# Two stacked transformer networks on one core: filler shares replanned, attention's output banks taken later, half down tiles stacked

## The chip, the core and the metric

The kernel runs on one core of one Trainium2 chip. The metric is device time of one execution in microseconds (us), smaller is better. The core has a matmul engine (TensorE; PE in the profile, its weight loads PEld), a vector engine (DVE), an activation engine (ACT), and DMA queues that SyncE (SP) issues to. Engines run their own instruction lists in order and meet at semaphores; the matmul engine too, so a matmul that waits holds up every matmul written behind it.

## The reference

256 tokens of 1024 features pass a first network of two layers and then a second one of two layers; a context of 256 tokens passes the second network beside them, up to the keys and values that the last attention reads. Cut to what matters:

```python
def first_block(x, ...):
    for i in range(2):
        x = layer_norm(ALPHA * x + 0.5 * swiglu(x, gate1[i], up1[i], down1[i]), ...)   # hidden width 2752
        x = layer_norm(ALPHA * x + hybrid_mixer(x, ...), ...)        # four kinds of attention
        x = layer_norm(ALPHA * x + 0.5 * swiglu(x, gate2[i], up2[i], down2[i]), ...)
        x = x + sigmoid(x @ ple_w_gate[i] + b) * (p[i] @ ple_w_proj[i])

def second_block(x, c, ctx, c_ctx, ...):
    for i in range(2):
        m_lat, m_ctx = silu(c) @ ada_w[i] + ada_b[i], silu(c_ctx) @ ada_w[i] + ada_b[i]   # 9 vectors each
        x   = x   + 0.5 * gt1 * swiglu_2(modulate(x,   g1, sh1, sc1), wi, wo)             # hidden width 2816
        ctx = ctx + 0.5 * cg1 * swiglu_2(modulate(ctx, g1, ch1, cs1), wi, wo)
        # i == 0: a conformer convolution (width 31) on x and on ctx
        # i == 1: windowed attention; x reads its own and the context's keys and values
        p = softmax(concat([s_win, s_ctx, sinks]))                     # one sink logit per head
        x = x + gt2 * y;  x = x + 0.5 * gt3 * swiglu_2(modulate(x, g3, sh3, sc3), wi, wo)
        # ctx does the same while i == 0
    return rmsnorm(x, final_g)
```

## The kernel before

Activations lie features by tokens in eight chunks of 128 features. Every large product is made in three matmuls of 128x128 weights on 256 tokens, `mm3` (L741): the weight tile and the input are each split into a rounded part and a rest (`split`, L625, one ACT copy and one DVE subtraction per 128x1024 tile), and the three products that matter are added in PSUM. Weights come from HBM as one packed tile per 24 matmuls.

**Streams.** The program is a set of generators. The main stream runs x through fifteen stages, and `self.phase` counts them: 1 to 4 are feed-forward 1, mixer, feed-forward 2 and gated projection (PLE) of layer 0 of the first network, 5 to 8 the same of layer 1; 9 is the second network's first feed-forward, 10 the front of its convolution, 11 the convolution's taps, norm and projection, 12 and 13 feed-forwards, 14 the attention, 15 the last feed-forward. Inside a mixer or the attention further streams of the same rank do heads in parallel. Two *filler* streams stand beside it: the context stream (`ctx_stream`, matmuls whose input is an `f` or `fh` buffer) and the ada stream (`ada`, L1028: 96 groups of four products, eight matmul records each, that read a 768 KB slab of `ada_w` from one of two buffers `a`). A third kind of work, the convolution's taps, is DVE work alone, put in wherever DVE would idle (`tap`).

**Who goes next** is decided before the program is built: `plan` runs all generators against a cost model (`Model`) and `choose` (L679) writes the list of steps, which the build replays. The main stream goes while its next matmul's operands are ready within 40 ns of the modelled clock; where it isn't, filler goes. Beside that, each microsecond of main work in stage k earns FILLS[k] us of credit (L37), which is spent on filler even though main work is ready. So FILLS moves filler out of one stage's bulk into it, and with it decides how much filler is left for the waits behind. The ada stream is held in layer 1 before group HOLD_G (L1052) until the attention starts.

**Half tiles.** The hidden width 2752 is 21.5 tiles. In the first network's feed-forwards the last piece has 64 rows; `ffn_main` (L786) multiplies it with weights cut to 64 rows (`k=rows` in `mm3`), three matmuls per output chunk, and goes between pieces of 128 and of 64 rows output pair by output pair.

**Attention.** `attention2` (L1702): three workers do eight head pairs. `scores` (L1738) takes two PSUM banks per half, adds the mask (DVE), exponentiates with a running sum (ACT), and exponentiates the sink of each half and head by itself. The output product accumulates in four of the eight PSUM banks, taken when the first pair (flag `a0`) is done.

Of the kernel before, what the change touches and what calls it, by code (L numbers as in the profile page):

```python
# [14 lines left out]
OP = mybir.AluOpType  # L15
# [21 lines left out]
FILLS = (0.25, 0.1, 0.05, 0, 0, 0.05, 0.08, 0, 0.5, 0.25, 0.08, 0.08, 0.05, 0.4, 0.25, 0.05, 0, 0.1)  # L37
# [7 lines left out]
HOLD_G = 5  # L45
# [7 lines left out]
TAP_SLACK = 400  # L53

# [228 lines left out]
class Model:  # L283


    def __init__(self):
        self.clock = [0.0] * 4
        self.table = None
        self.busy = [0.0] * 4
        self.cold, self.window, self.activity = True, 0, 0.0  # L290

# [37 lines left out]
    def pe(self, cost, rows, reads, writes):  # L329

        start = max(self.clock[PE], self.need(PE, reads, writes))
# [61 lines left out]
class WTile:  # L393
# [3 lines left out]
    def h(self, j, m=128):  # L397
        return self.hi[:, j * 128:j * 128 + m]

    def l(self, j, m=128):  # L400
        return self.lo[:, j * 128:j * 128 + m]
# [54 lines left out]
class Prog:  # L456
# [84 lines left out]
    def mms(self, group, cost=None, rows=None):  # L541

        if self.model:
            yield self.model.need(PE, [v for g in group for v in g[1:3]], [g[0] for g in group])
        else:
            yield 0.0
        self.mms_now(group, cost, rows)

    def mms_now(self, group, cost=None, rows=None):
# [8 lines left out]
        m.pe(cost or sum(m.pe_cost(l, r, r.n) for _, l, r, _, _ in group), rows, reads, writes)  # L558
# [182 lines left out]
    def mm3(self, ps, t, j, xh, xl, start, stop, m=128, k=128):  # L741
        wh, wl = t.h(j, m), t.l(j, m)
        if k != 128:
            wh, wl, xh, xl = wh[:k], wl[:k], xh[:k], xl[:k]
        yield from self.mms([(ps, wh, xh, start, False), (ps, wh, xl, False, False), (ps, wl, xh, False, stop)])
# [56 lines left out]
    def ffn_main(self, R, xs, kind, l, acc):  # L802
# [3 lines left out]
        def down(ps):  # L806
# [3 lines left out]
            for b in range(4):  # L810
                for (f, th, rows, key), t in zip(ps, ts):
                    for n in (2 * b, 2 * b + 1):
                        yield from self.mm3(acc[b][:, n % 2], t, n, th[:, 0], th[:, 1], f == 0 and n % 2 == 0,
                                            f == NFB - 1, k=rows)
# [4 lines left out]
        for f in range(NFB):  # L819
# [7 lines left out]
            if uk is None:  # L827
# [6 lines left out]
                self.hidden(ps[:64, 0], u[:64], False, s[:64], h[:64], hh[:64], hl[:64])  # L834
# [11 lines left out]
    def ffn_keys(self, kind, l, f):  # L846
        r0 = f * 128
        if kind in ("ffn1", "ffn2"):
            g, u, d = kind + "_w_gate", kind + "_w_up", kind + "_w_down"
            if f == NFB - 1:  # L850
# [4 lines left out]
                return tuple(key), None, rows_tile(d, l, r0, DFF), 64  # L855
# [176 lines left out]
    def ada(self, l):  # L1032
# [26 lines left out]
        for g in range(6):  # L1059
# [3 lines left out]
            for kc in range(8):  # L1063
# [4 lines left out]
                                     for j in range(4)], 704.0)  # L1068
# [52 lines left out]
    def mixer(self, l, xs, acc):  # L1121
# [221 lines left out]
        def softmax(P, sm, ng, qk, cost=930.0):  # L1343
# [38 lines left out]
        def values(T, O, cols, start=True, stop=True):  # L1382
# [3 lines left out]
                                   for i in range(2)], 860.0)  # L1386
# [31 lines left out]
        def fox(w, j):  # L1418
# [14 lines left out]
            yield from softmax(P, sm, ng, qk, 1760.0)  # L1433
# [298 lines left out]
    def attention2(self, x, xs, G):  # L1732
# [24 lines left out]
        def scores(w, c, P):  # L1757
# [4 lines left out]
            for qb in range(2):  # L1762
# [9 lines left out]
                yield from self.mms(group, 1160.0, 128)  # L1772
                for p, ps in enumerate(pss):
# [26 lines left out]
        def pair(w, c):  # L1800
# [5 lines left out]
            for p in range(2):  # L1806
# [3 lines left out]
                                  T[:, p, kb], kb == 0, kb == 3) for kb in range(4) for p in range(2)], 2230.0)  # L1810
# [254 lines left out]
```

## Time and profile before

| | |
|---|---|
| time, median of 3 runs | 2953.66 us (2950.4 to 2954.9) |
| the profiled execution | 2951.42 us, its span 2949.3 us |
| mean granted matmul clock | 0.976 of full |
| PE busy, PEld busy | 2847.2 us (97%), 2689.1 us (91%) |
| DVE, ACT busy | 1960.3 us (66%), 1407.1 us (48%) |
| DMA | 553.91 MB, 188 GB/s over the span |

All times below are counted from the span's start. A stretch's granted clock is 1.00 at 2.4 GHz and 0.50 at 1.2 GHz; a mean between them is a mix of the two.

### The profile page before, as it was taken

The numbers are of one execution on the slowest core, as the hardware profiler recorded it, in microseconds if no ns is written. First come the engines' busy times: TensorE is split into PE (matmuls) and PEld (weight loads), VectorE is DVE, ScalarE is ACT, GpSimd is POOL, SyncE is SP. The second block draws the span as 40 slices with busy tenths as digits, with TensorE's granted clock in tenths as the row PEclk, the third lists the DMA queues.
The fourth block names the chain that finished last, engine by engine and source line by source line (L and its number), as shares of the span: only waits on it lengthen the run. The fifth ranks groups of instructions, "written<-read, shape, count | busy, mean of one in ns | idle before, by whom it ended". The sixth has DMA issues, their size and how long they took to land.

```text
span 2949.3 us, 55792 instructions
## 1 busy us (share of the span) xinstructions
PE 2847.2 (97%) x23184; PEld 2689.1 (91%) x23184; DVE 1960.3 (66%) x3423; ACT 1407.1 (48%) x2212; POOL 0.2 (0%) x4
## 2 busy tenths in 40 slices
PE   8999999999999999999899989999999999988898
PEld 8999879999999877999799879989999999966898
DVE  5456776557555676755899989987556555666554
ACT  4345445445444544544544444446445444554543
POOL 0000000000000000000000000000000000000000
PEclk9999999999999999999899989999999999989999
DMA  8766645654565555555655665565655555531453
GB/s 289 276 228 209 210 156 173 201 186 162 194 193 164 201 209 194 177 186 183 229 181 184 211 205 198 179 201 190 198 181 177 196 185 187 200 133 45 142 190 111
DMA packets 152845, 553.91 MB, mean 188 GB/s; under 512 B 16272, under 2 KB 26256, under 8 KB 152464
## 3 DMA queue, kind: packets, MB, share of 16 engines
q1 hardware_dynamic: 151728, 548.30, 55.9%
q8 instruction: 182, 2.98, 0.4%
q10 hardware_dynamic: 864, 2.05, 0.2%
q14 instruction: 71, 0.58, 0.1%
HBM read 549.24 MB, written 1.05 MB: 187 GB/s over the span
## 4 chain that ended last, share of the span: by engine, by line
PE 87%; DVE 5%; DMA 4%; ACT 3%; issue 1%; SPq 0%; ACTq 0%; DVEq 0%
PE p L553 86%; DMA a<-ada_w 2%; DVE w L481 1%; PE p L570 1%; ACT k L475 1%; DMA r<-W 1%; DVE m L481 1%; ACT w L475 1%; DVE p L517 1%; ACT m L475 1%; ACT f L475 0%; DMA m_cE<-lam 0%; DVE k L488 0%; DVE m L496 0%; DMA a<-phi_v 0%
## 5 line engine op out<-in xcount | busy, mean ns | idle before, releaser
L553 PE MATMUL p<-m,w 128*128 128x256 f32 x10896 | 1393.1, 284 | 9.1 <-ACT w L475 5.7
L553 PEld LDWEIGHTS p<-m,w 128*128 128x128 f32 x10896 | 1339.6, 190 | 34.2 <-issue 13.1
L481 DVE TENSOR_TENSOR w<-r,w 128x1024 fp32r<-128x1024 f32 (+1 forms) x884 | 1057.9, 1216 | 427.0 <-ACT w L475 416.1
L475 ACT ACTIVATE w<-r 128x1024 fp32r<-128x1024 f32 (+1 forms) x884 | 901.2, 1045 | 435.0 <-PE p L553 336.5
L553 PE MATMUL p<-k,w 128*128 128x256 f32 x4224 | 553.0, 283 | 0.0
L553 PEld LDWEIGHTS p<-k,w 128*128 128x128 f32 x4224 | 524.7, 188 | 8.8 <-issue 4.4
L553 PE MATMUL p<-f,w 128*128 128x256 f32 x3600 | 489.9, 286 | 0.0
L553 PEld LDWEIGHTS p<-f,w 128*128 128x128 f32 x3600 | 454.9, 191 | 10.4 <-issue 4.0
L475 ACT ACTIVATE k<-p 128x256 f32<-128x256 f32 (+1 forms) x200 | 80.6, 403 | 421.8 <-PE p L553 420.9
L553 PE MATMUL p<-fh,w 128*128 128x256 f32 x1776 | 243.3, 284 | 0.2 <-ACT k L475 0.2
L553 PEld LDWEIGHTS p<-fh,w 128*128 128x128 f32 x1776 | 223.7, 190 | 7.2 <-issue 4.2
L481 DVE TENSOR_TENSOR k<-k,p 128x256 f32<-128x256 f32 x176 | 74.0, 420 | 210.3 <-ACT k L475 210.0
L481 DVE TENSOR_TENSOR k<-k,k 128x256 fp32r<-128x256 f32 (+1 forms) x176 | 74.9, 426 | 85.3 <-ACT k L475 85.3
L475 ACT ACTIVATE k<-k 128x256 fp32r<-128x256 f32 (+1 forms) x176 | 73.7, 419 | 108.4 <-DVE k L481 108.4
L553 PE MATMUL p<-a,csf 128*32 128x384 f32 x768 | 93.0, 569 | 30.6 <-DMA a<-ada_w 30.4
L475 ACT ACTIVATE m<-m 128x512 f32<-128x512 f32 (+4 forms) x121 | 64.2, 548 | 81.3 <-DVE m L481 39.9
L496 DVE SCALAR_TENSOR_TENSOR m<-m,vec,m 128x241 f32<-128x241 f32 (+14 forms) x240 | 100.6, 472 | 0.0
L496 DVE SCALAR_TENSOR_TENSOR f<-fh,vec,f 128x241 f32<-128x241 f32 (+14 forms) x240 | 99.9, 473 | 0.0
L553 PEld LDWEIGHTS p<-a,csf 128*32 128x32 f32 x768 | 16.9, 115 | 57.0 <-DMA a<-ada_w 40.3
L475 ACT ACTIVATE k<-p,m_qn 128x128 f32<-128x128 f32 x96 | 39.0, 419 | 60.3 <-DVE m_qn L517 60.3
L517 DVE CUSTOM_DVE_ANT_0 p<-p,masksb 128x128 f32<-128x128 f32 (+2 forms) x128 | 56.0, 453 | 14.9 <-PE p L553 13.3
L475 ACT ACTIVATE f_sq<-p 128x256 f32<-128x256 f32 x66 | 24.9, 378 | 82.3 <-PE p L553 81.9
(219 smaller groups left out, 1428.3 us busy)
## 6 DMA issues: line engine op xcount, KB each, us to landing
r<-W SPq DMA_DIRECT2D x876, 512.0 KB, 4.2
a<-ada_w SPq DMA_DIRECT2D x96, 768.0 KB, 4.9
a<-phi_k SPq DMA_DIRECT2D x8, 512.0 KB, 6.5
a<-phi_v SPq DMA_DIRECT2D x8, 512.0 KB, 4.0
m<-xT SPq DMA_DIRECT2D x4, 256.0 KB, 4.9
r<-W SPq DMA_DIRECT2D x8, 128.0 KB, 4.7
f<-ctxT ACTq DMA_DIRECT2D x1, 1024.0 KB, 10.0
out<-m SPq DMA_DIRECT2D x4, 256.0 KB, 2.5
```

The lines of the kernel that those rows point to most:

```text
L475: self.nc.scalar.activation(out, in_, func, **kw)
L481: self.nc.vector.tensor_tensor(out=out, in0=a, in1=b, op=op)
L496: self.nc.vector.scalar_tensor_tensor(out, a, s, b, op0=op0, op1=op1)
L517: self.nc.vector.tensor_tensor_reduce(ps, ps, mask, -1.0, 3e38, OP.add, OP.min, ng)
L553: self.nc.tensor.matmul(out, l, r, start=start, stop=stop, skip_group_check=True)
L570: self.nc.tensor.transpose(out, in_, ident[:k, :k])
```

## The change

It does four things. The diff is cut to them; lines that only pass arguments or lower a cost in the model are left out.

```diff
-FILLS = (0.25, 0.1, 0.05, 0, 0, 0.05, 0.08, 0, 0.5, 0.25, 0.08, 0.08, 0.05, 0.4, 0.25, 0.05, 0, 0.1)
+FILLS = (0.25, 0.196, 0.025, 0.0, 0, 0.05, 0.08, 0.8, 0.25, 0.02, 0.18, 0.112, 0.18, 0.49, 0.175, 0.05, 0, 0.1)
-HOLD_G = 5
+HOLD_G = 4
+A2_ACC = 2
+TURN = 95.0
...
+    def turned(self, mode):
+
+        t = TURN if mode != self.mode else 0.0
+        self.mode = mode
+        return t
...
-        m.pe(cost or sum(m.pe_cost(l, r, r.n) for _, l, r, _, _ in group), rows, reads, writes)
+        mode = (min(g[1].t.shape[1] for g in group), min(-(-g[1].n // 32) for g in group))
+        turn = m.turned(tuple(x if x < 3 else 4 for x in mode))
+        m.pe(turn + (cost or sum(m.pe_cost(l, r, r.n) for _, l, r, _, _ in group)), rows, reads, writes, need)
...
-                        yield from self.mm3(acc[b][:, n % 2], t, n, th[:, 0], th[:, 1], f == 0 and n % 2 == 0,
-                                            f == NFB - 1, k=rows)
+                        o, last = acc[b][:, n % 2], f == NFB - 1
+                        if rows == 128:
+                            yield from self.mm3(o, t, n, th[:, 0], th[:, 1], f == 0 and n % 2 == 0, last)
+                        else:
+
+                            yield from self.mms([(o, t.h(n), th[:, 0], False, False), (o, t.l(n), th[:, 1], False, last)])
...
-                self.hidden(ps[:64, 0], u[:64], False, s[:64], h[:64], hh[:64], hl[:64])
+                self.hidden(ps[:64, 0], u[:64], False, s[:64], h[:64], hh[:64], hh[64:])
+                self.act(hl[:64], h[:64])
+                self.ts(hl[64:], u[:64], 0.0, None, OP.mult)
...
-                return tuple(key), None, rows_tile(d, l, r0, DFF), 64
+                return tuple(key), None, rows_tile(d, l, r0, DFF) + (piece(d, l, r0, DFF, 0, D, 64),), 64
...
-                    self.act(es[:, p, qb:qb + 1], sk[p], AF.Exp, bias=n1)
+                    self.tt(es[:, p, qb:qb + 1], sk[p], n1, OP.add)
                     R.banks.put(ps)
+            self.act(es, es, AF.Exp)
...
             if c == 0:
+                yield from self.until(f"a{A2_ACC}")
                 for _ in range(4):
                     acc.append((yield from R.bank()))
```

1. **Half pieces stacked.** The 64 weight rows are packed twice, one below the other, and the input's rounded part and its rest fill the two halves of one 128-row operand. Two matmuls of 128 rows do what three of 64 did: 64 stand for 96 in the four feed-forwards, 32 fewer in all. One ACT copy and one DVE multiplication are added to each of the four.
2. **Sinks merged.** Per head pair one ACT exponential of four numbers stands for four of one, and four DVE additions of one column are new.
3. **Banks later.** The four banks of the output product are taken after the third pair (`a2`) is done.
4. **Replanning.** New shares, HOLD_G, and a model that charges 95 ns where the matmuls' tiling changes. No work is added or dropped by it, but nearly every step of every engine stands elsewhere. Filler that stands in the stretches which the prediction speaks of, counted from the program's order (ctx in matmul records, ada in groups):

| stretch | ctx before | ada before | ctx after | ada after |
|---|---|---|---|---|
| stage 6, from the last differential scores to the last forgetting head | 145 | 14 | 174 | 11 |
| stages 7 to 8, from the layer norm's first sum to PLE's first product | 75 | 3 | 0 | 8 |
| stage 10, from stage 9's last product to the convolution's first | 0 | 6 | 147 | 2 |
| stage 11, its start to the context's next gate product | 192 | 9 | 0 | 2 |
| stage 14, last query product to first scores | 175 | 5 | 0 | 0 |
| stage 14, first scores to last output product | 0 | 1 | 0 | 13 |

Matmul engine, the layer norm between stage 7 and stage 8, before. `con` as second operand sums a norm's squares, `m_nr` is its result being transposed, `f` is the context stream, `a` with `csf` the ada stream, `m` with `w` the main stream:

```order
L553 MATMUL p_362_15675<-f_6_12476,w_832_15544 128x256
L553 MATMUL p_362_15675<-f_6_12476,w_831_15543 128x256
L553 MATMUL p_362_15675<-f_7_12477,w_831_15543 128x256
L553 MATMUL p_362_15675<-f_6_12476,w_832_15544 128x256
L553 MATMUL p_303_12550<-a_70_12621,csf 32x384 x4
L553 MATMUL p_303_12550<-a_71_12690,csf 32x384 x4
L570 MATMUL p_363_15745<-con,m_nr_15732 128x128 x2
L553 MATMUL p_303_12550<-a_72_15766,csf 32x384 x4
L553 MATMUL p_365_15806<-m_44_15777,w_833_15607 128x256
```

And the same norm after; `m_41` with `con` are its four partial sums:

```order
L562 MATMUL p_361_15860<-m_41_15858,con 128x256 x2
L562 MATMUL p_362_15868<-a_66_15869,csf 32x384 x4
L562 MATMUL p_361_15860<-m_41_15858,con 128x256 x2
L562 MATMUL p_362_15868<-a_67_15875,csf 32x384 x4
L562 MATMUL p_361_15860<-m_41_15858,con 128x256 x2
L562 MATMUL p_362_15868<-a_68_15887,csf 32x384 x4
L562 MATMUL p_361_15860<-m_41_15858,con 128x256 x2
L562 MATMUL p_362_15868<-a_69_15900,csf 32x384 x4
L562 MATMUL p_362_15868<-a_70_15913,csf 32x384 x4
L562 MATMUL p_363_15936<-con,m_42_15859 128x2 x4
L562 MATMUL p_362_15868<-a_71_15941,csf 32x384 x4
L581 MATMUL p_364_15970<-con,m_nr_15957 128x128 x2
```

The context's products have left this norm; ada groups stand one by one between its steps.

Matmul engine, the norm at the head of stage 10, before: from stage 9's last product (`k` with `w`) to the convolution's first (`m` with `w`):

```order
L553 MATMUL p_384_16507<-k_259_18477,w_984_18480 128x256
L553 MATMUL p_379_16314<-a_81_16294,csf 32x384 x4
L553 MATMUL p_379_16314<-a_82_16315,csf 32x384 x4
L553 MATMUL p_379_16314<-a_83_18675,csf 32x384 x4
L553 MATMUL p_404_18670<-con,m_51_18651 128x2 x4
L570 MATMUL p_405_18687<-con,f_row_16312 128x128 x3
L553 MATMUL p_379_16314<-a_84_18681,csf 32x384 x4
L570 MATMUL p_406_18712<-con,m_nr_18699 128x128 x2
L553 MATMUL p_379_16314<-a_85_18719,csf 32x384 x4
L553 MATMUL p_379_16314<-a_86_18725,csf 32x384 x4
L553 MATMUL p_407_18763<-m_52_18731,w_985_18512 128x256
```

And after, around the transposes of `m_nr`; `fh` is the context's convolution output:

```order
L562 MATMUL p_410_18879<-fh_8_17416,w_995_18761 128x256
L562 MATMUL p_410_18879<-fh_9_17417,w_995_18761 128x256
L562 MATMUL p_410_18879<-fh_8_17416,w_996_18762 128x256
L581 MATMUL p_409_18856<-con,m_nr_18843 128x128 x2
L562 MATMUL p_410_18879<-fh_8_17416,w_995_18761 128x256
```

The context's projection fills this norm from end to end, and the ada groups have left it but for two.

Matmul engine, the attention's first scores, before (`m_of` and `fh` are keys, `m_68` queries, `f_19` with `con` a transposed probability block):

```order
L553 MATMUL p_586_29903<-fh_22_29765,m_68_28986 128x256
L553 MATMUL p_562_29055<-a_112_29746,csf 32x384 x4
L553 MATMUL p_587_29916<-m_of_28987,m_68_28986 128x256
L553 MATMUL p_588_29917<-m_of_28987,m_68_28986 128x256
L553 MATMUL p_587_29916<-fh_22_29765,m_68_28986 128x256
L553 MATMUL p_588_29917<-fh_22_29765,m_68_28986 128x256
```

And after:

```order
L562 MATMUL p_568_29358<-a_103_29847,csf 32x384 x4
L562 MATMUL p_590_29875<-m_of_29348,m_68_29347 128x256
L562 MATMUL p_591_29876<-m_of_29348,m_68_29347 128x256
L562 MATMUL p_590_29875<-fh_22_29132,m_68_29347 128x256
L562 MATMUL p_591_29876<-fh_22_29132,m_68_29347 128x256
L562 MATMUL p_568_29358<-a_104_29881,csf 32x384 x4
L581 MATMUL p_593_29908<-con,f_19_29785 128x128 x4
L562 MATMUL p_595_29941<-a_105_29913,csf 32x384 x4
L581 MATMUL p_596_29949<-con,f_19_29785 128x128 x4
```

Before, one ada group (`a_112`) stands in the whole attention; now one stands before nearly every step of the first round.

## Rows read from the trace of the kernel before

**Rows 1.** Busy times of the page.

```profile
PE 2847.2 (97%) x23184; PEld 2689.1 (91%) x23184; DVE 1960.3 (66%) x3423; ACT 1407.1 (48%) x2212; POOL 0.2 (0%) x4
```

**Rows 2.** Windows, one a stage: stretch, length, PE busy, granted clock, DMA share, GB/s.

```profile
246.00:492.00 246.00, 237.66 (x1910) 0.99 0.55 184
492.00:708.00 216.00, 216.00 (x1789) 1.00 0.58 188
965.00:1201.00 236.00, 220.96 (x1734) 0.96 0.59 198
1653.50:1717.70 64.20, 58.12 (x470) 0.92 0.63 218
1717.70:2029.00 311.30, 296.14 (x2418) 0.95 0.60 200
2524.60:2733.30 208.70, 188.35 (x1393) 0.93 0.36 121
```

**Rows 3.** What PE waited for: us in total, times, longest us.

```profile
PE p L553 <- DMA a<-ada_w: 30.4, 19, 3.8
PE p L553 <- DVE p L529: 8.6, 2, 5.0
```

**Rows 4.** Groups of PE instructions by form: busy us, mean ns; idle before.

```profile
L553 PE MATMUL p<-k,w 128*128 128x256 f32 x4128 | 539.3, 283 | 0.0
...
L553 PE MATMUL p<-k,w 64*128 64x256 f32 x96 | 15.6, 295 | 0.0
```

**Rows 5.** Windows: length, busy of PE, PEld, DVE, ACT, POOL; clock, DMA share, GB/s.

```profile
1010.00:1020.00 10.00, 5.03 (x39) 3.47 (x38) 8.67 (x23) 4.29 (x6) 0.00 (x0) 0.83 0.38 121
1087.00:1134.00 47.00, 37.54 (x265) 18.28 (x263) 33.43 (x138) 22.14 (x73) 0.00 (x0) 0.82 0.63 205
1394.00:1416.00 22.00, 18.25 (x142) 14.77 (x140) 17.18 (x37) 10.15 (x19) 0.00 (x0) 0.97 0.44 158
1446.00:1460.00 14.00, 9.64 (x59) 3.94 (x58) 11.12 (x32) 4.52 (x10) 0.00 (x0) 0.72 0.71 234
1653.00:1670.00 17.00, 10.91 (x71) 4.58 (x71) 14.90 (x45) 6.83 (x14) 0.00 (x0) 0.71 0.76 266
1717.00:1724.00 7.00, 3.29 (x31) 1.16 (x29) 5.15 (x9) 3.83 (x8) 0.00 (x0) 0.83 0.62 222
1749.00:1769.00 20.00, 12.30 (x77) 5.96 (x70) 15.39 (x38) 9.47 (x17) 0.00 (x0) 0.67 0.71 231
2606.00:2621.00 15.00, 9.98 (x67) 5.11 (x67) 9.45 (x24) 7.27 (x14) 0.00 (x0) 0.72 0.77 267
2632.00:2662.00 30.00, 23.72 (x143) 15.25 (x143) 21.54 (x65) 16.57 (x47) 0.00 (x0) 0.83 0.05 18
2662.00:2733.00 71.00, 63.03 (x445) 48.44 (x446) 45.70 (x118) 33.12 (x86) 0.00 (x0) 0.93 0.16 53
```

**Rows 6.** PE over time at stage 10's head: start, length, engine, [idle before].

```profile
1653.50 1.50 PE L553 MATMUL p<-a,csf 128*32 128x384 f32 x16
1658.75 0.85 PE L553 MATMUL p<-a,csf 128*32 128x384 f32 x8 [3.76 <-DMA a<-ada_w]
```

**Rows 7.** The same view of DVE before stage 6's first compression product.

```profile
1006.88 0.23 DVE L481 TENSOR_TENSOR m_hT<-m_cE 128x64 f32<-128x64 f32 x1 [3.36 <-DMA m_cE<-lam]
...
1015.16 0.27 DVE L529 MEMSET p<- 128x256 f32 x1
```

**Rows 8.** The same view of PE, the norm between stages 7 and 8.

```profile
1394.21 1.13 PE L553 MATMUL p<-m,con 128*128 128x256 f32 x4
...
1413.84 1.16 PE L553 MATMUL p<-m,w 128*128 128x256 f32 x6
```

**Rows 9.** The same view of DVE, one small step in the attention.

```profile
2636.53 0.16 DVE L496 SCALAR_TENSOR_TENSOR m_qn<-vec,m_qn 128x1 f32<-128x1 f32 x1
```

**Rows 10.** The same view of ACT, a sink's exponential there.

```profile
2636.15 0.28 ACT L475 ACTIVATE m_nv<-vec,m_qn 128x1 f32<-128x1 f32 x1
```

**Rows 11.** The ada slabs' transfers, issue to landing.

```profile
DMA to landing us min/median/max: 3.4/4.9/9.3
```

More of the change, by code (lines that the diff above doesn't have):

```diff
@@ L290, in __init__ @@
         self.cold, self.window, self.activity = True, 0, 0.0
+        self.mode = None
     def need(self, e, reads, writes):
@@ L327, in dve, with pe @@
         self.run(DVE, fixed + rate * outs[0].n, ins, outs)
-    def pe(self, cost, rows, reads, writes):
-        start = max(self.clock[PE], self.need(PE, reads, writes))
+    def turned(self, mode):
+        t = TURN if mode != self.mode else 0.0
+        self.mode = mode
+        return t
+    def pe(self, cost, rows, reads, writes, need=None):
+        start = max(self.clock[PE], self.need(PE, reads, writes) if need is None else need)
         self.turn(start)
@@ L395, in __init__, with h, l @@
         self.prog, self.hi, self.lo = prog, hi, lo
[L397 to L401, printed above, removed]
+    def h(self, j):
+        return self.hi[:, j * 128:j * 128 + 128]
+    def l(self, j):
+        return self.lo[:, j * 128:j * 128 + 128]
     def done(self):
@@ L541, in mms, with mms_now @@
     def mms(self, group, cost=None, rows=None):
+        need = 0.0
         if self.model:
[L544 to L549, printed above, removed]
+            need = self.model.need(PE, {id(v): v for g in group for v in g[1:3]}.values(), {id(g[0]): g[0] for g in group}.values())
+        yield need
+        self.mms_now(group, cost, rows, need)
+    def mms_now(self, group, cost=None, rows=None, need=None):
         m = self.model
@@ L737, in choose, with mm3 @@
                 credit -= used
[L741 to L744, printed above, removed]
+    def mm3(self, ps, t, j, xh, xl, start, stop):
+        wh, wl = t.h(j), t.l(j)
         yield from self.mms([(ps, wh, xh, start, False), (ps, wh, xl, False, False), (ps, wl, xh, False, stop)])
@@ L1067, in ada @@
                 yield from self.mms([(ps[32 * j:32 * j + 32], self.csf[:, kc], t[:, j], kc == 0, kc == 7)
-                                     for j in range(4)], 704.0)
+                                     for j in range(4)], 740.0)
                 self.ada_slots.put(t)
@@ L1341, in mixer, with softmax @@
         seg = (slice(0, 128), slice(128, 384))
-        def softmax(P, sm, ng, qk, cost=930.0):
+        def softmax(P, sm, ng, qk, cost=760.0):
             pss = []
@@ L1385, in values @@
                                 + [(o[i][:, 128:256], V[:, 1, cols(i):cols(i) + 64], T[:, i, 256:384], False, stop)
-                                   for i in range(2)], 860.0)
+                                   for i in range(2)], 710.0)
         def finish(src, c):
@@ L1432, in fox @@
             P = yield from self.take(R.wk, (128, 2, 384))
-            yield from softmax(P, sm, ng, qk, 1760.0)
+            yield from softmax(P, sm, ng, qk, 1420.0)
             scaled(P, sm)
@@ L1771, in scores @@
                         group.append((pss[p][:, a:a + 256], q[b, c, qb * 128:qb * 128 + 128], kk[b], True, True))
-                yield from self.mms(group, 1160.0, 128)
+                yield from self.mms(group, 970.0, 128)
                 for p, ps in enumerate(pss):
@@ L1809, in pair @@
             yield from self.mms([(O[64 * p:64 * p + 64], (v, self.vc2)[kb // 2][:, kb % 2, (2 * (c // 4) + p) * 64:][:, :64],
-                                  T[:, p, kb], kb == 0, kb == 3) for kb in range(4) for p in range(2)], 2230.0)
+                                  T[:, p, kb], kb == 0, kb == 3) for kb in range(4) for p in range(2)], 1785.0)
             self.act(OH[:, c], O)
```

## Prediction, made before the changed kernel was timed

> **What bounds the kernel.** The page's busy line comes first: PE is busy for 97% of the span and no other engine for more than 66% [rows 1], so only time in which PE idles, or works at the low clock, can be gained without removing matmuls. The windows by stage say where that time lies: a plain feed-forward, 492 to 708, is busy throughout at a granted clock of 1.00, while the mixer of layer 1 (965 to 1201), the convolution (1653 to 2029) and the attention (2524 to 2733) lose 15.0, 6.1, 15.2 and 20.4 us of PE's time and run at 0.92 to 0.96 [rows 2]. PE's own waits name the causes: 30.4 us in 19 waits for ada slabs, 8.6 us in two waits for a cleared PSUM tile [rows 3]. Last, narrow windows around the norms and the attention, where the main chain runs through DVE and ACT and PE has only filler to do [rows 5].
>
> How I price a stretch: its length less PE's busy time is idle. A granted clock c over a length L means that L(1-c) us of full-speed work were lost at most, less where slow time was idle anyway. The price lies between the idle and the sum of both. Filler that is moved is neither gain nor loss by itself, since its matmuls are done somewhere in any case; what counts is the idle that it covers or uncovers.
>
> **A. Stacked half pieces: 7 us.** The 96 matmuls of 64 rows keep PE busy for 15.6 us, 0.163 each; 4128 full ones of the same operands take 539.3 us, 0.131 each [rows 4]. 64 full ones cost 8.4, so 7.2 us go, with the changes of tiling that the 64-row runs bring. If only the 32 matmuls counted it would be 32 x 0.131 = 4.2; 9 at most, if the return to 128 rows costs the next matmul something too. The added ACT copy and DVE multiplication stand beside the previous piece's 24 down products, 24 x 0.131 = 3.1 us of cover; without it each of the four would cost about 0.3, the size of an ACT step such as that in [rows 10].
>
> A rule of the Trainium skill speaks against A. TensorEngine Tiling (Array Packing), section Performance Considerations, says that a contraction of 64 or less is a case for row tiling, up to twice as fast. By it 96 half-height matmuls would be worth 48 full ones, 6.3 us, and the change would lose 2 us instead; the sum below would be 42. The row of this case shows 0.163 for one, slower than a full one [rows 4], so the trace does not bear the rule out here, where all 96 read the same half of the rows.
>
> **B. Head of stage 10: 8 us.** 17 us hold 10.91 of PE work at clock 0.71 [rows 5]: 6.1 idle, 4.9 more at most through the clock. PE issues two ada groups and then stands 3.76 us for the third slab [rows 6]. In the new order 147 context matmuls (19 us at 0.131) fill the norm. I take 8 of 6 to 11.
>
> **C. Head of stage 11: 13 us.** In 1717 to 1724 and 1749 to 1769 PE idles 3.7 and 7.7 us at clocks 0.83 and 0.67 [rows 5]: 11.4, up to 19.2. It is the context's own norm: main has nothing but taps, the context stream is between two products, and only ada is left. In the new order that norm stands inside the convolution's front products, and stage 11 starts with two ada groups, whose slabs lie ready in the two buffers, and then with the next gate products. Price 15, less 2 for what is left of it. The like place near 1956 stays as it is and costs nothing more.
>
> **D. The context's tail in stage 14: 6 us.** 2606 to 2621 is the same picture, 5.0 idle, up to 9.2 [rows 5]. In the new order the context's keys and values are made at the end of stage 13 and in stage 14's first norm, so this stretch goes.
>
> **E. The attention itself: 10 us.** 2632 to 2733 has 6.3 and 8.0 us idle at 0.83 and 0.93 [rows 5], 14.3 to 24.4. In the first 30 us there are no matmuls to fill with but one ada group; now 12 more, 0.78 us each (16 matmul records take 1.50 and the next row's start is as far off [rows 6]), 9.4 us of work that need not be done elsewhere. A slab takes 4.9 us to land [rows 11] and there are two buffers, so a group every 2.5 us, 30 us for 12: just the length of the round, so some will make PE wait and hold scores behind them. I take 4. In the later 71 us the banks that are kept back until `a2` let two workers hold scores while a third transposes; I take 6 of 8 to 13. Bounds for both: 4 lost to 20 gained.
>
> **F. Mixer of layer 1: 12 us.** The products of the compression wait 4.97 of the 10 us from 1010 for a PSUM tile that DVE clears [rows 3, 5], because DVE stood 3.36 us for a small parameter's transfer and then had a row of small steps in front of the clearing [rows 7]. The compression products now stand some 50 projection matmuls later, since both buffers hold ada slabs when their weights are asked for: 6 us, idle and clock, go. It would come back only if the projections behind were held by the same DVE work. From 1087 to 1134 9.5 us idle at 0.82, up to 18 [rows 5]: the context's norm lay in the middle of the softmaxes; it moves ahead into the projections, ctx goes from 145 to 174 and ada from 14 to 11. Since the ada groups that stay wait as before, I take 6 of 0 to 13.
>
> **G. Mixer of layer 0: 3 us.** Its stage idles 8.3 us [rows 2], 3.6 of them by the wait for the cleared tile, which keeps its place here (8.6 less 4.97 [rows 3]); more context products stand in the softmaxes. 3 of 0 to 4.7.
>
> **H. Norm between stages 7 and 8: 5 us lost.** From the first partial sum to PLE's first product it takes 19.6 us [rows 8], with 75 context matmuls and 3 ada groups in it, and PE idles 3.8 in the window [rows 5]. Now the context stream waits for taps and 8 ada groups stand there, at 2.5 us a piece, 20 us: the norm is as long as before, but holds 8 x 0.78 + 26 sums of some 0.13 = 9.6 us of work. Idle rises to some 10, and the chain hides a part of the rest: 5 lost, 2 to 9.
>
> The clock makes H worse if it falls. With ctx in the norm the granted clock was 0.97, in the ada-filled stretch 1446 to 1460 it was 0.72 [rows 5]. The skill's TensorE: Matmul & The Clock Gate, section HAM oscillation, says that waits between short bursts send the array back to its slow state, so that each burst begins slow. The two rows agree with it; by the rule the loss at H is its bound, 9, and the sum 47.
>
> **I. The rest: 3 us lost.** The attention gets 32 DVE additions of 0.16 us [rows 9], 5.1 us on the engine that paces the first round, and loses 24 ACT steps of 0.28 [rows 10], which paced nothing; 2 lost, 0 to 5. The order has some changes of tiling more outside the half pieces: 1.
>
> **Sum.** 7 + 8 + 13 + 6 + 10 + 12 + 3 - 5 - 3 = 51 us. The profiled execution took 2951.4, 2.1 outside its span and 2.2 under the median of 2953.7; its sum gives 2900, and the same 51 off the median give 2902.7, which I round to 2902.
>
> **Rivals.**
> *Paid back by ada.* D, E and the softmax part of F are replaced by ada groups that PE waits for. Then 6, 10 and 6 go from the sum and H is 8: 26 us, 2928. For it: the largest of PE's waits is that for ada [rows 3], and E's groups need all of their round. Against it: 36 ada groups stand in waiting places after and 38 before, so their waits need not grow.
> *Idle is only moved.* The context matmuls that cover B, C and G were covering something else. Then A and 6 of F stay, less H and I: 5 us, 2949. For it: the number of filler matmuls is the same. Against it: they come out of stage 12 to 14, where PE is dense, or from the context's tail.
> *Slower by ada waits.* At H, in F's softmaxes and in E 32 groups stand one by one before steps of the main chain, and PE runs in order: each late slab delays the norm or the scores. It decides once the 32 wait 1.6 us more on average than counted (51 / 32), as long as the mean of the waits seen, 30.4 / 19; at 2.0 each the time is 2953.7 + 13 = 2967. Against it: the longest wait is 3.8 and most groups came without one.
> *All upper bounds.* 7 to 20 us more in B to F: about 2868.
>
> **Chances.** The forecast 0.64, with its own range 2882 to 2918; paid back 0.22; only moved 0.06; slower 0.05; upper bounds 0.03. A change under 0.2% (5.9 us) cannot be told from none here. Faster by more holds the forecast, paid back, the upper bounds and a sixth of "only moved": 0.90; within 0.05, slower 0.05. The range 2874 to 2936 leaves out the last two rivals, the upper bounds and the worst of "paid back".
>
> **What would show it.** A: no 64-row matmuls with `k` and `w`. B, C, D: no ada wait above 1 us at the heads of stages 10 and 11, clock 0.95 or more there, and no context norm between the query products and the scores. E: scores to last output product in 90 to 97 us with 13 ada groups, against 101. F: the wait for a cleared tile is seen once, where there were two. H: clock under 0.9 and 8 to 12 us idle between stage 7 and 8. The forecast is wrong if PE's idle time falls by less than 25 us, or if the ada waits grow past 45 us.

## The result, and the profile after

The changed kernel takes 2905.16 us (median, 2903.5 to 2914.0), the kernel before, on the same chip, 2952.13: a ratio of 0.9846 (95% interval 0.9824 to 0.9868), 47 us less. Forecast were 2902 and 51 less. The profiled execution of that series was its longest, with a span of 2912.2. A second series gave 2904.01, ratio 0.9834 (0.9821 to 0.9848), and a profile with a span of 2902.2, which stands nearer the median; the rows below are of this second profile. Of the 10 us between the two, 3 to 4 lie in the mixer of layer 0, 3 in stage 11, the rest in pieces of 2 or less.

The busy line of the page (what each engine worked, share of the span, instructions):

```profile
PE 2812.8 (97%) x23152; PEld 2668.6 (92%) x23152; DVE 1961.6 (68%) x3460; ACT 1403.4 (48%) x2192; POOL 0.2 (0%) x4
```

Against [rows 1] PE is busy for 34.4 us less, and its idle time falls from 102.1 to 89.4 us, by 12.7 alone. So most of the gain is in the *busy* time, where two things are: matmuls that are gone or run faster, and matmuls that no longer run at the low clock. The mean granted clock went from 0.976 to 0.985; with the forecast's own measure, length times (1 - clock), 70.8 us fell to 43.5. Counted in the trace, the stretches at 1.2 GHz hold 105.5 us of PE's busy time before and 63.6 after; there full matmuls start 0.214 us apart, elsewhere 0.118 (medians), so an estimate at half speed is 52.7 us lost before and 31.8 after, 21 less.

Windows, one a stage (stretch, length, PE busy and its records, PEld, DVE, ACT, POOL, granted clock, DMA share, GB/s): the mixer of layer 0, the plain feed-forward, the mixer of layer 1, stages 7 and 8, the convolution's stages 10 and 11, and stage 14:

```profile
261.10:493.50 232.40, 223.53 (x1821) 197.24 (x1820) 169.34 (x418) 117.49 (x240) 0.00 (x0) 1.00 0.54 186
493.50:706.70 213.20, 212.93 (x1774) 212.52 (x1773) 126.09 (x165) 101.41 (x139) 0.00 (x0) 1.00 0.57 187
963.60:1188.30 224.70, 211.38 (x1696) 181.92 (x1694) 165.31 (x424) 113.59 (x236) 0.00 (x0) 0.98 0.57 190
1188.30:1404.50 216.20, 206.32 (x1692) 196.35 (x1689) 194.76 (x373) 95.67 (x140) 0.00 (x0) 0.98 0.59 191
1404.50:1440.00 35.50, 33.79 (x268) 30.28 (x269) 28.44 (x45) 21.87 (x35) 0.00 (x0) 0.91 0.68 242
1650.80:1720.60 69.80, 69.80 (x594) 68.66 (x593) 61.31 (x112) 40.96 (x62) 0.00 (x0) 1.00 0.55 181
1720.60:2018.60 298.00, 290.49 (x2406) 277.83 (x2404) 266.29 (x498) 144.09 (x208) 0.00 (x0) 0.98 0.61 204
2528.40:2689.00 160.60, 145.52 (x1117) 114.93 (x1115) 113.83 (x282) 76.64 (x153) 0.00 (x0) 0.94 0.46 155
```

For each row length less PE is the idle time; against [rows 2] it falls from 15.0 to 13.3 in the mixer of layer 1, from 6.1 to nothing in stage 10, from 15.2 to 7.5 in stage 11 and from 20.4 to 15.1 in stage 14. Stage 7 goes the other way. The same two rows of the kernel before:

```profile
1200.70:1413.10 212.40, 208.87 (x1735) 205.93 (x1735) 123.00 (x159) 102.09 (x140) 0.00 (x0) 1.00 0.56 180
1413.10:1446.30 33.20, 32.99 (x264) 29.94 (x264) 26.39 (x40) 20.89 (x34) 0.00 (x0) 0.95 0.67 249
```

Idle 3.7 before, 11.6 after.

What PE waited for (in total, times, longest), to be read beside [rows 3]:

```profile
PE p L562 <- DMA a<-ada_w: 26.4, 18, 3.0
...
PE p L562 <- DVE p L538: 3.3, 1, 3.3
PE p L562 <- DVE m L511: 2.9, 1, 2.9
```

The ada waits are about as before (32.4 in the first profile of the changed kernel). Of the two waits for a cleared tile one is left; the third row is new, and the experiments come back to it.

The form of the half pieces is gone from the groups [rows 4]:

```profile
L562 PE MATMUL p<-k,w 128*128 128x256 f32 x4192 | 548.2, 282 | 0.0
```

Narrow windows that answer [rows 5]: the compression and the softmaxes of layer 1, the norm between stages 7 and 8, the heads of stages 9, 10 and 11, the context's second norm in stage 11, the norm of stage 14, the attention's first 30 us and its rest:

```profile
1008.00:1018.00 10.00, 7.11 (x40) 6.45 (x39) 9.42 (x14) 2.12 (x2) 0.00 (x0) 0.84 0.74 245
1060.00:1110.00 50.00, 42.81 (x359) 28.27 (x359) 37.09 (x137) 24.95 (x64) 0.00 (x0) 0.97 0.61 209
1380.30:1408.90 28.60, 17.28 (x103) 6.49 (x100) 21.68 (x58) 6.97 (x14) 0.00 (x0) 0.80 0.76 252
1440.00:1453.00 13.00, 8.92 (x54) 3.27 (x53) 9.44 (x28) 3.66 (x8) 0.00 (x0) 0.69 0.70 229
1650.80:1667.80 17.00, 17.00 (x151) 15.92 (x149) 16.31 (x35) 7.71 (x11) 0.00 (x0) 1.00 0.39 125
1720.60:1727.60 7.00, 5.52 (x47) 3.11 (x45) 5.71 (x15) 4.16 (x7) 0.00 (x0) 1.00 0.84 285
1915.00:1932.00 17.00, 11.41 (x70) 4.58 (x69) 12.33 (x34) 7.70 (x16) 0.00 (x0) 0.63 0.67 225
2528.40:2547.00 18.60, 16.01 (x125) 13.37 (x124) 15.98 (x36) 12.34 (x23) 0.00 (x0) 0.92 0.54 191
2586.10:2616.10 30.00, 24.14 (x194) 13.11 (x193) 23.24 (x76) 14.20 (x35) 0.00 (x0) 1.00 0.71 237
2616.10:2689.00 72.90, 66.27 (x501) 51.34 (x497) 51.73 (x146) 34.24 (x75) 0.00 (x0) 0.91 0.28 95
```

The head of stage 10 is the cleanest: 17 us without a gap at the full clock, where the kernel before had 6.1 idle at 0.71. The softmaxes stand at 0.97 against 0.82 with nearly as much idle time (7.2 for 9.5). The norm between stages 7 and 8 is 28.6 us long, 11.3 of them idle, at 0.80. In it PE waits for ada seven times, and its groups start 3.4 us apart (eight from the first row to the last below):

```profile
PE p L562 <- DMA a<-ada_w: 9.1, 7, 2.6
```

```profile
1383.94 0.85 PE L562 MATMUL p<-a,csf 128*32 128x384 f32 x8
...
1407.44 1.51 PE L562 MATMUL p<-a,csf 128*32 128x384 f32 x8 [1.39 <-DMA a<-ada_w]
```

### The profile page after: what moved, and what is told of

Same layout as the page of the kernel before. It is cut to its first block, busy times and chain, and to the rows that moved or that the text cites. A ratio compares the mean times of both kernels' runs of the same rounds, so it can differ in the third digit from the quotient of the medians.

```text
span 2912.2 us, 55723 instructions
## 1 busy us (share of the span) xinstructions
PE 2817.0 (97%) x23152; PEld 2671.7 (92%) x23152; DVE 1962.0 (67%) x3460; ACT 1403.3 (48%) x2192; POOL 0.2 (0%) x4
## 3 DMA queue, kind: packets, MB, share of 16 engines
HBM read 549.24 MB, written 1.05 MB: 189 GB/s over the span
## 4 chain that ended last, share of the span: by engine, by line
PE 79%; DVE 11%; DMA 4%; ACT 4%; issue 2%; SPq 0%; ACTq 0%; DVEq 0%
PE p L562 78%; DVE w L490 3%; DMA a<-ada_w 3%; DVE m L505 2%; DVE m L490 1%; PE p L581 1%; ACT w L484 1%; DVE p L526 1%; ACT m L484 1%; ACT k L484 1%; DMA r<-W 1%; DMA a<-phi_v 0%; DVE f_sq L490 0%; ACT fh L484 0%; DMA m_cE<-lam 0%
## 5 line engine op out<-in xcount | busy, mean ns | idle before, releaser
L562 PE MATMUL p<-a,csf 128*32 128x384 f32 x768 | 92.1, 561 | 34.0 <-DMA a<-ada_w 32.4
L505 DVE SCALAR_TENSOR_TENSOR m<-m,vec,m 128x241 f32<-128x241 f32 (+14 forms) x240 | 100.7, 474 | 0.0
```

The lines of the kernel that those rows point to most:

```text
L505: self.nc.vector.scalar_tensor_tensor(out, a, s, b, op0=op0, op1=op1)
L562: self.nc.tensor.matmul(out, l, r, start=start, stop=stop, skip_group_check=True)
```

## The experiments

Times are medians; ratios are to the kernel before, run on the same chip.

**The changed kernel again.**

> The changed kernel once more, for a second profile and for the baseline of the other runs. Its first profiled execution spans 2912 us, 7 to 9 us more than its other executions, so the profile may hold a stretch that is not typical. Theory: the steps keep their sizes (in the first profile the idle time of PE fell by 7 us and its busy time by 30 us) and the missing 8 us turn up in one stage; then the time is 2905 +- 3 and one stage of the new profile is shorter by 5 us or more. Rival: the 8 us are spread over all stages, and no stage differs by more than 3 us.

It took 2904.01 us. Neither picture holds in full: two stages (the mixer of layer 0 and stage 11) give 6 to 7 of the 10 us, the rest is spread. Rows of one profile that differ by 3 us a stage prove nothing here.

**Stacking alone, in the old order.** The plan is made as before; only what is built differs:

```
 if rows == 128 or self.planning:  (as before, three products)
+else:
+    yield from self.mms([(o, t.h(n), th[:, 0], False, False), (o, t.l(n), th[:, 1], False, last)])
```

> The kernel before, in its own old order, with only the half pieces stacked (64 matmuls of full height instead of 96 of half height, one ACT copy and one DVE multiplication more in each of four half pieces). Theory, term A of the prediction: 7 us less (4.2 to 9), so 2945 against 2952 for before. Rival 1: only the number of matmuls counts, 4 us less, 2948. Rival 2: the added ACT and DVE steps hold the down products, no gain or a loss, 2952 or more.

It took 2940.57, ratio 0.9964 (0.9951 to 0.9976): 10.6 us less, 7.1 to 14.5. One of the four half pieces with the full piece beside it, first in the kernel before, then stacked (window, length, PE busy, further columns as above):

```profile
681.86:688.20 6.34, 6.34 (x43) 5.38 (x43) 3.31 (x5) 1.89 (x3) 0.00 (x0) 1.00 0.54 171
```

```profile
676.61:680.68 4.07, 4.07 (x36) 4.07 (x35) 3.54 (x5) 1.39 (x3) 0.00 (x0) 1.00 0.52 170
```

The same work takes 2.27 us less; all four together, with the records next to them, 9.5. Eight matmuls less account for 8 x 0.131 = 1.0 of it. The other 1.2 belong to eight changes between half and full rows: behind each, whichever way it goes, two matmuls start some 0.08 us late (205 to 227 ns apart, 114 to 126 elsewhere). That is the upper bound of the forecast's term A ("9 at most, if the return to 128 rows costs the next matmul something too"), and the term should have stood there. By the prediction's estimate, the rule of the Trainium skill that it weighed (TensorEngine Tiling (Array Packing), section Performance Considerations) would have made this a loss of 2; the run shows 10.6 gained, in a kernel whose 64-row matmuls all read the same half of the rows.

**The attention's banks taken early again.** The line `yield from self.until(f"a{A2_ACC}")`, the wait for the third pair's flag `a2`, is left out; outside the attention the order stays.

> The changed kernel without the wait for the second pair, so that the attention's four output banks are taken before the first output product as in the kernel before; everything outside the attention stays in the order of the changed kernel. Theory, the later part of term E: 6 us slower than the changed kernel (2 to 8), 2911, with PE's idle time in the attention up by 4 to 6 us. Rival: the banks are not what holds the scores, within 2 us of the changed kernel, 2905.

It took 2909.34, ratio 0.9864 (0.9850 to 0.9878), 5 us slower than the changed kernel. From the first scores to the last output product, with early and with late banks:

```profile
2583.10:2691.90 108.80, 93.99 (x691) 64.43 (x690) 75.71 (x221) 48.55 (x110) 0.00 (x0) 0.95 0.38 129
```

```profile
2586.10:2689.00 102.90, 90.41 (x691) 64.44 (x690) 74.97 (x221) 48.44 (x110) 0.00 (x0) 0.93 0.41 136
```

The same 691 records take 5.9 us more, where three profiles of the changed order (the third is that of lam early, below) give 102.7 to 103.2. The theory stands in size and not in kind: only 2.3 of the 5.9 are idle time, for 4 to 6 expected. The rest is busy time at a clock that is no lower (0.95 for 0.93); what it is stays open.

**The sinks' exponentials one by one.**

```
-self.tt(es[:, p, qb:qb + 1], sk[p], n1, OP.add)      (one addition a row)
+self.act(es[:, p, qb:qb + 1], sk[p], AF.Exp, bias=n1)
-self.act(es, es, AF.Exp)                             (the merged exponential)
```

> The changed kernel with the sinks' exponentials taken one by one again (32 ACT steps more in place of 8 merged ones, 32 DVE additions less). Theory, term I: DVE paces the first round of the attention, so this is 2 us faster than the changed kernel (0 to 5), 2903. Rival: ACT paces it, so this is 3 to 7 us slower, 2908 to 2912.

It took 2908.90, ratio 0.9856 (0.9843 to 0.9870), 5 us slower by medians with intervals that overlap, as the rival said, and still this does not decide: the planner ordered the attention anew for it (it takes 104.0 us), and the rows of scores themselves came faster. ACT's exponentials of three rows of scores, merged sinks first, then split (start, length, idle before):

```profile
2599.48 0.69 ACT L484 ACTIVATE f<-p,m_qn 128x512 f32<-128x512 f32 x1 [0.28 <-DVE m_qn L505]
...
2600.53 0.69 ACT L484 ACTIVATE f<-p,m_qn 128x512 f32<-128x512 f32 x1 [0.28 <-DVE m_qn L505]
...
2601.59 0.69 ACT L484 ACTIVATE m<-p,m_qn 128x512 f32<-128x512 f32 x1 [0.28 <-DVE m_qn L505]
```

```profile
2599.19 0.68 ACT L484 ACTIVATE f<-p,m_qn 128x512 f32<-128x512 f32 x1
...
2600.04 0.69 ACT L484 ACTIVATE f<-p,m_qn 128x512 f32<-128x512 f32 x1
...
2600.91 0.69 ACT L484 ACTIVATE m<-p,m_qn 128x512 f32<-128x512 f32 x1
```

With merged sinks a row comes every 1.05 us and ACT stands 0.28 for DVE in each; split, every 0.86 and ACT does not stand in these rows. DVE paces the rows, as term I had it. The last experiment settles it.

**Shares alone, and everything but the shares.** The kernel after with the old `FILLS`, and the kernel before with the new `FILLS` and `HOLD_G = 4`.

> The changed kernel with the filler shares of the kernel before (the other edits, the group from which ada waits for the attention and the planner's costs stay as changed). Theory: the shares carry the terms B, C, D, F and G less H; stacking (11 us measured by itself) and the attention's banks and sinks (5 each) stay, so 2952 - 21 = 2931, about 27 us slower than the changed kernel, with the ada waits back at the heads of stages 10 and 11. Rival, idle is only moved: the shares are worth under 8 us, 2912 or less.

> The kernel before with the new filler shares and with ada waiting for the attention from its fifth group of layer 1 on, and none of the other edits. Theory: the shares and the two parts of the attention's change add up, so this stands 27 us under the kernel before, 2925, with stage 10 and the two heads of stage 11 without long ada waits. Rival: they belong together (without the later banks the ada groups in the attention hold the scores, and the old planner's costs put the groups elsewhere), and it gains 15 us or less, 2937 or more.

The first took 2945.19, ratio 0.9973 (0.9963 to 0.9983): 8 us less than before, for 21 expected, where stacking by itself gave 10.6. The second took 2937.47, ratio 0.9946 (0.9932 to 0.9959): 16 less, for 27 expected. 8 and 16 are not 47: the parts belong together, as the rival for the second had it. Stage 10's head, with old shares and then with new ones:

```profile
1652.50:1669.50 17.00, 12.63 (x76) 6.11 (x76) 14.55 (x43) 8.17 (x16) 0.00 (x0) 0.70 0.81 292
```

```profile
1664.00:1681.00 17.00, 17.00 (x148) 16.21 (x147) 15.95 (x35) 8.05 (x11) 0.00 (x0) 1.00 0.38 125
```

Term B hangs on the shares alone and is there in full. What is missing in the second kernel is stage 14: with the ada groups in the attention and the banks taken early, its window up to the next stage gives 26.2 us idle at 0.87, against 18.1 at 0.94 in the changed kernel. From the first scores to the last output product the same 691 records take 118.1 us, for 102.9:

```profile
2605.20:2723.30 118.10, 102.66 (x691) 69.61 (x690) 70.88 (x189) 52.40 (x134) 0.00 (x0) 0.86 0.35 118
```

So 15.5 of the shares, 10.6 of stacking and 15.2 of this attention make 41 of the 47, if they add; the other 6 are not traced. The first kernel has B's head back (4.4 us idle at 0.70) but not that of stage 11, which idles 1.7 us in its first 7 as the changed kernel does (1.5). It has 3 us more idle time in stage 1 and 4 more in stage 9 than the kernel before (7.0 for 3.9, 8.3 for 4.4); why the planner's order came out so was not traced.

**Quarter slabs: what are ada waits worth?** A quarter of each slab is transferred and read four times.

```
-self.load(t, w.rearrange("p (j c) -> p j c", j=4))
+self.load(t[:, 0], w.rearrange("p (j c) -> p j c", j=4)[:, 0])     (matmuls read t[:, 0])
```

> The changed kernel, in its own order, with only a quarter of each ada slab transferred, 192 KB for 768, and the group's four matmuls reading that quarter; three quarters of the ada weights are left out of the result. PE waited 26 to 32 us for slabs in the two profiles. Theory (these waits are paid in full, above all the 10 us between stages 7 and 8): 20 us or more faster than the changed kernel, 2884 or less. Rival (paid back: in the norms and the softmaxes main waits for DVE and ACT anyway): those waits turn into waits for DVE and ACT, and it is 12 us or less faster, 2892 or more.

> The kernel before with the same quarter slabs. It tells whether the change pays part of its gain back through ada. Theory (not paid back): it gains as much from them as the changed kernel does, within 4 us. Rival (paid back): the changed kernel, which puts more groups one by one before steps of the main chain, gains at least 6 us more from them than the kernel before does.

They took 2887.87, ratio 0.9779 (0.9765 to 0.9792), and 2940.93, 0.9960 (0.9948 to 0.9973): 16 and 12 us less. A slab now lands in 2.4 us, not 5.0, and the wait for it is all but gone, from 26.4 us in the changed kernel. The waits of that kernel with quarter slabs:

```profile
PE p L562 <- DVE m L490: 11.5, 8, 3.7
PE p L581 <- DVE m_nr L505: 7.7, 4, 2.3
...
PE p L562 <- DMA a<-ada_w: 1.7, 3, 1.2
```

Of 24.7 us of wait that vanish, 16 reach the time: both pictures are half right. All of PE's waits for DVE grow from 28.9 to 41.1 us (the sum over the view's rows), since DVE's chain is late next. The kernel before loses as much wait, 30.4 us down to 5.9, and gains 12. The 16 may hold more than these waits, since 57 MB less are moved: ACT's waits for raw weight tiles fall too, from 52.2 to 33.7 us. By medians the change pays 4 us more to its slabs than the kernel before, between the two answers, under 4 and over 6; the intervals of the three ratios allow from nothing to 11, so this does not decide. The attention is no shorter with quarter slabs (104.1 us): late slabs do not pace it.

**The norm between stages 7 and 8: fewer groups, or context.** The planner lets ada no further in stages 7 and 8 after a few groups; or the share of stage 5 is 0.

> The changed kernel with at most three ada groups in the norm between stages 7 and 8, as the kernel before has there, and nothing in the place of the others; all stages up to that norm are as in the changed kernel, and those behind it are ordered anew, so only stages 7 and 8 are compared. Theory (PE runs in order, and the late slabs hold the sums of the norm): from the last product of stage 7 to the first of stage 8 it takes 20 us, as in the kernel before, against 28 to 29 in the changed kernel. Rival (DVE and ACT set the length of the norm and the groups only fill it): 26 us or more.

> The changed kernel with the filler share of stage 5 set to zero, so that some 70 context matmuls move from the second feed-forward and 24 from the mixer of layer 1 to the norm between stages 7 and 8, and four ada groups from that norm into the mixer. Term H says that the norm is dear because only ada groups are left for it. Theory: stages 7 and 8 together lose 6 us or more of their idle and slow time (they are 251.7 us long in the second profile of the changed kernel, with 11.6 idle and 6.8 lost to the clock) and the mixer of layer 1 gives back less than half of it, so 2901 or less. Rival: the mixer pays it back in full through more ada waits, 2904 or more.

The first left one group, not three, in this window, ahead of the norm's sums, where the changed kernel has nine. It then takes 21.6 us for 28.6:

```profile
1387.40:1409.00 21.60, 9.69 (x38) 5.76 (x36) 18.50 (x51) 4.25 (x9) 0.00 (x0) 0.74 0.34 122
```

So eight groups lengthen the norm by 7.0 us: the theory, 20, is near and the rival, 26 or more, is out. The quarter slabs say why, since they leave the order as it is and take the ada wait in this norm from 9.1 us to 0.3. With all nine groups the same stretch then takes 23.2:

```profile
1378.70:1401.90 23.20, 16.22 (x102) 6.61 (x100) 20.37 (x55) 4.99 (x10) 0.00 (x0) 0.81 0.33 102
```

5.4 of the 7.0 are late slabs; the groups' matmuls cost 1.6 there, and 8 x 0.78 = 6.3 elsewhere. But slabs are not the whole of it: with one group PE still idles 11.9 of 21.6 us, for the chain of sums, DVE and ACT. The kernel before, with 75 context matmuls in 19.7 us, idled 3.5. What is lost is the cover, and the late slabs come on top. (The whole took 2932.04; everything behind is ordered anew.)

The second took 2914.84, ratio 0.9872 (0.9856 to 0.9887), slower by 10, and is no test of that: the context matmuls it freed went into stage 7's own products, and the norm still held eight groups and no context. It shows the price of taking them from the mixer of layer 1, which then has 17.9 us idle at 0.95, not 13.3 at 0.98.

**Lam early.** In the changed kernel's own order the small transfer is issued at the mixer's start:

```
 self.phi_next.extend((l, a, q) for a in range(2) for q in range(4))
+lp = R.tmp((128, 2, 2, 32), "cE", 1)
+self.load(lp, self.io["lam"][l], "scalar")
```

> The changed kernel in its own order, with one edit: the transfer of the small parameter lam, for which DVE stands 2.8 us in the mixer of layer 0 and 4.6 us in that of layer 1, is issued at the mixer's start and no longer beside its use. Theory (this stall is what delays the compression's cleared tile in layer 0 and, in layer 1, the copy that frees the projections behind it, so term F was paid back there): PE's waits of 3.3 us at 306 and 2.9 us at 1011 go, and the time falls by 4 to 8 us, to 2898. Rival: DVE's other steps there (the halves of the weights) hold PE just as long, within 2 us of 2904.

Why this was tried: DVE in the mixer of layer 1, and the products of PE that come after, in the changed kernel:

```profile
1000.54 0.22 DVE L490 TENSOR_TENSOR m_hT<-m_cE 128x64 f32<-128x64 f32 x1 [4.62 <-DMA m_cE<-lam]
```

```profile
1014.49 1.72 PE L562 MATMUL p<-m,con 128*128 128x256 f32 x4 [2.89 <-DVE m L511]
```

With lam early the same two rows, and the tile's landing (3.6/3.8/4.0 us when issued beside its use; there the DMA moved 313 and 149 GB/s in the 4 us from the issue on, at the mixer's start 18 and 30):

```profile
996.61 0.22 DVE L490 TENSOR_TENSOR m_hT<-m_cE 128x64 f32<-128x64 f32 x1
...
1012.96 1.13 PE L562 MATMUL p<-m,con 128*128 128x256 f32 x4 [0.98 <-DVE m L511]
...
DMA to landing us min/median/max: 1.7/1.8/1.9
```

In the mixer of layer 0 the wait of 3.3 us falls to 0.8. It took 2897.17, ratio 0.9808 (0.9787 to 0.9829): 7 us under the changed kernel by medians, with intervals that overlap. The mechanism is shown by the rows: the wait of layer 1 that the change removed, 5.0 us, came back as one of 2.9 from the same stall of DVE. The forecast had named that case ("only if the projections behind were held by the same DVE work") and given it nothing.

**Lam early, and one sink addition a pair.** As above, with DVE's one step on lam's exponential moved behind the small gate steps, and

```
+self.tt(es, both[:, :, None].to_broadcast([128, 2, 2]), ng, OP.add)   (once a pair, for four)
 self.act(es, es, AF.Exp)
```

> The changed kernel in its own order with lam's transfer at the mixer's start, the one DVE step that needs its exponential moved behind the row of small gate steps (DVE stood 2.7 us for that exponential in layer 1 once lam came early), and the four sink additions of a pair of heads made as one addition ahead of the merged exponential. Theory (in the first round DVE paces the rows of scores: they come every 1.05 us with the added steps, while they came every 0.86 us where the sinks had ACT steps of their own): the rows come every 0.88 us, what ACT needs, the attention shrinks from 102.8 us by 2 to 5, and the whole is 3 to 7 us under the kernel with lam early alone, 2890 to 2894. Rival (the late ada slabs pace the round): the attention stays within 1 us of 102.8 and the whole within 2 us of 2897.

It took 2891.87, ratio 0.9801 (0.9787 to 0.9814): better than both kernels, 13 us under the changed one with intervals that do not overlap. Against lam early alone it is 5 us by medians and 2 by the ratios, with intervals that overlap; there the attention's own rows decide. The attention, and three rows of scores:

```profile
2578.60:2676.20 97.60, 87.07 (x692) 62.04 (x690) 71.30 (x197) 48.51 (x110) 0.00 (x0) 0.98 0.43 144
```

```profile
2591.04 0.69 ACT L484 ACTIVATE f<-p,m_qn 128x512 f32<-128x512 f32 x1
...
2591.90 0.69 ACT L484 ACTIVATE f<-p,m_qn 128x512 f32<-128x512 f32 x1
...
2592.76 0.69 ACT L484 ACTIVATE m<-p,m_qn 128x512 f32<-128x512 f32 x1
```

A row every 0.86 us, and 97.6 us for 102.9 (103.2 with lam early alone). So 24 DVE additions of 0.16 us, 3.8 us in all, cost 5.3 in this order: 2.0 of it is idle time, and 3.3 is busy time, with the clock up from 0.93 to 0.98. The moved step gave nothing: DVE then stood 2.9 us for the next step of ACT's queue.

## Why the prediction was right, and where its steps were not

The time was right, 47 us gained of 51 forecast, but two errors in the working cancel: too much idle time was to go, and too little was expected of the clock. To that extent the hit is luck.

- **What is lost to the clock was priced too low.** Terms B to D took 6.5 of the 16.9 us that their rows allow for it (8 - 6.1, 15 - 11.4 and 6 - 5.0); E and the softmaxes of F took less than their idle time alone. Measured: 12.7 us of idle time went, 10.6 came from stacking, and the rest of the 47 us between the two spans, some 24, is left for the clock, whose bound fell by 27. Two counts bear that out. Stacking alone, with the changed kernel's 23152 matmul records in the old order, has a busy time of 2837.0 us, and the changed kernel 2812.8, 24.2 less; and the estimate from the stretches at 1.2 GHz gives 21. Changes of tiling, which could also slow the same matmuls, are about as many in both (294 and 298). The forecast's own test, "wrong if PE's idle time falls by less than 25 us", failed while the time was right: it asked the wrong quantity. In the softmaxes the clock rose from 0.82 to 0.97 with nearly the idle time of before (7.2 for 9.5 us), and with 359 matmul records in 50 us for 265 in 47.
- **A** (7): mis-sized, 10.6 by the time and 9.5 by the rows. The change of tiling was mentioned and priced at the half matmuls alone.
- **B** (8): right; 6.1 idle and up to 5 of clock are gone, with the shares alone too.
- **C** (13): stage 11 lost 7.7 less to idle and up to 10 less to the clock. Its head is 1.5 idle for 3.7, in one ada wait that is over the 1 us of the forecast's sign. The place that was to cost "nothing more" got dearer: 5.6 idle at 0.63 near 1920, for 3.8 at 0.78 in the kernel before.
- **D and E** (16): the idle time of stage 14 falls by 5.3, its clock loss by up to 5. D is partly given back in the norm of stage 14, 2.6 us idle at 0.92, for none at 1.00. In E the attention takes 102.9 us against 101.3 and holds 13 ada groups instead of one, 12 x 0.78 = 9.4 of work done on the way: 7.8 gained for 10. The text's "90 to 97 us" did not follow from its own terms, which give 101.3 + 9.4 - 10 = 100.7.
- **F** (12): mis-sized, 1.7 of idle, which is within the 3 us by which two profiles differ, and up to 5 of clock. The step "6 us, idle and clock, go" failed: the wait moved to the projections behind, and lam early showed why.
- **G** (3): up to 2.5 through the clock, less 0.5 of idle; within the same 3 us, so not shown.
- **H** (-5): mis-sized. Idle time rises by 7.9 and up to 5.8 come through the clock, 8 to 14 for a bound of 9. The mechanism was the forecast's, groups that wait for slabs, but a group takes 3.4 us, not 2.5. A slab lands in 5.9 us there (median of eight), not 4.9, and its buffer is free for the next only when its matmuls, some 0.8, are done; half of that sum, for two buffers, is 3.4 (an estimate). So the norm is not "as long as before" but 28.6 us long, 5.4 of them by late slabs. Beside that the context's cover is missing: with one group PE idles 11.9 us in this norm. The norm's clock was 0.80, with quarter slabs 0.81, with one group 0.74. This agrees with the section HAM oscillation of the Trainium skill's TensorE: Matmul & The Clock Gate, that waits between short bursts send the array back to its slow state.
- **I** (-3): the sinks alone lose 5.3, just past the range that was given for them; the 1 us for other changes of tiling was not measured by itself.
- **All upper bounds**: 2868 does not follow from "7 to 20 us more", which off 2902 gives 2882 to 2895.

Of the rivals, "paid back by ada" has at most a small part: by medians slabs cost the changed kernel 16 us and the kernel before 12, so 4 of the gain would go there, and the intervals do not tell that from nothing. "Idle is only moved" holds for F and partly for D, and for H above all: of 20.8 us of idle time that left the mixer of layer 1 and stages 10, 11 and 14, 7.9 turned up in stages 7 and 8, whose context matmuls now cover other waits.

## What to carry to other kernels

Price a stretch of short idle pieces nearer to idle plus clock than to idle alone, if filler is to stand in it from end to end, as stage 10's head shows; and ask of every removed wait which engine's stall stood behind it, for that stall serves the next instruction. An operation merged on an engine with time to spare is no gain if it adds steps to the one that paces. Edits that a planner turns into one order don't add up: the shares gave 16 us alone, all the rest without them 8, together 47. And before a wait is priced by its landing, count how long the buffer is held too: a group in the norm came every 3.4 us, not every 2.5.

## What was not expected of the hardware

A matmul of 64 rows between full ones costs not only its own 0.163 us: with the change there and back a run of 24 half and 18 other matmuls took 6.34 us, against 4.07 for 16 full ones and the same others. The same small transfer landed in 1.8 us when issued at the mixer's start, with 18 and 30 GB/s moved beside it, and in 3.8 beside its use, with 313 and 149. Waits of 26.4 us for transfers, nearly all taken away, were worth 16.
